# A two-layer streaming encoder: the attention accumulator of layer 1 emptied in mid-step, two cache copies and a table of biases moved to other stages

## The chip, the cores and the metric

The kernel runs on 1 core of one Trainium2 chip, as one launch. The metric is the device time of that launch in microseconds (us). The engines are called PE (TensorE), DVE (VectorE), ACT (ScalarE), POOL (GpSimd) and SP (SyncE, which only issues DMAs here); PEld is PE's loading of weights. [...]

## The reference

One inference step of a two-layer encoder over a prompt of 2048 positions and a sample of 64 positions with caches; model width 1024. Each layer is `h + rms(W_out(gated mixer(rms(h))))`.

- Layer 0 has two head groups. A is latent attention over all earlier chunks. B is attention in a band of 9 chunks of 64 positions, with a bias by clipped relative distance (a table of 8 heads x 257). Each output is multiplied by the SiLU of its gate columns, and both go into one output projection.
- Layer 1 (C) is attention in a window of 128 positions, rounded to chunks, with 16 query heads on 2 key heads, a sink per head, partial rotation and a SiLU gate.

```
o_b = _band_prompt(q_b, k_b, v_b, B_PAST_CHUNKS, B_SCALE, rel_table=rel_table)
state = (c_new, kr_new, bk, bv)      # the sample's: bk, bv = the last 512 rows of [cache, new]
o = _band_prompt(q, k, v, C_PAST_CHUNKS, C_SCALE, sinks=sinks)
return h + _rms((o * jax.nn.silu(g)) @ w_out, post_g), state
```

Of the sample's new B caches (512 rows of keys, 512 of values), 448 rows are the old caches' rows 64 to 511, unchanged. Inputs and outputs are in float32.

## The kernel before

Products are made as three matmuls of split values: a value is a high part (rounded by ACT as it empties a PSUM bank: `copy`, L211) and a low part (what is left, made by DVE: `lo_of`, L214, the "low pass"). So almost each PSUM bank is read first by ACT, then by DVE.

The program has five phases, one after another: the projections of layer 0 (phase 1, in two halves of the positions), group A's attention (2), group B's (3), the projections of layer 1 (4) and its attention (5). Output projections of a layer run beside the attention, as jobs `J` that a step pumps: `J.proj` makes the products (L964), `tail` (L985) scales by the norm (the "z pair", two DVE operations at L995) and adds the residual on POOL (L1003). The order of the work is the Tile scheduler's in phase 1 and in the first 8 steps of phase 5 (`NAUTO5`). From step 8 on PE, DVE, ACT and SP follow the order in which the code is written (`manual`, L168).

**Phase 1.** Chunks of 384 positions are loaded as x tiles of 128 rows (L253), squared on ACT (L255), scaled on DVE (L264), transposed on PE (L268) and emptied into X (L211, L214). Weights come in pieces (L226), split by ACT (L227) and DVE (L228). In the first half, after the load of W_ukv, `biases_by_distance` (L293) loads the table `rel`, stretches it on DVE (L297), stores it to DRAM (sE1, L298) and has a DMA repeat it for 128 partitions from DRAM to DRAM (sE, L299, 3072 KB). Phase 3 reads sE. At the end of phase 1 (L597) two DMAs copy the 448 unchanged rows of each B cache from DRAM to DRAM, 896 KB each. The Tile scheduler had put all of these into the first 25 us. SP issues all these DMAs; it goes round 8 semaphores, so each DMA waits until the one 8 before it has landed.

**Phase 5.** A unit is a block of 128 queries with one key group g and one parity e of heads (4 query heads); a block has four units, (0,0), (0,1), (1,0), (1,1), so 64 units in all. The blocks go in the order 8 to 15, 0 to 7. Block 0 has one key tile, the others two. `step(n)` (L1897) runs three units at different stages: scores and masks of unit n+2 (`start`: PE L1705, DVE L1708), exponentials of unit n+1 (ACT L1717), transpositions of unit n's probabilities (`turn`, PE L1726, one for each key tile b, with `copy` and `low` into PT), and the product with the values of unit n-1 (`av`, PE L1733) into the accumulator `acc`, one PSUM bank. `out` (L1813) empties it: ACT copies the lower half (tbm, L211), DVE adds the upper half (OT, L1823). For a unit (0,0), `out` first pumps jobs until at most one block is open, and takes one of the two OT buffers. After unit (1,1) `gate` (L1735) transposes the reciprocal sums (PE L1755, into the same two PSUM banks `t` as the turns), multiplies (DVE L1757, POOL L1763), and makes the operand MM of the output projection (ACT L211, then POOL's subtraction L1770).

Of the kernel before, what the change touches and what calls it, by code (L numbers as in the profile page):

```python
# [110 lines left out]
def kernel(ctx, tc, a, o, upto=5):  # L111
# [3 lines left out]
    dma = nc.sync.dma_start  # L115
# [115 lines left out]
    def mm3(ps, lhs, rhs, kt):  # L231

        n = 3 * kt
        j = 0
        for k in range(kt):
            for x, y in TERMS:
                nc.tensor.matmul(ps, lhs(x, k), rhs(y, k), start=(j == 0), stop=(j == n - 1))  # L237
                j += 1
# [38 lines left out]
    def phase1():  # L277
        with ExitStack() as st:
# [14 lines left out]
            def biases_by_distance():  # L293

                e8 = tb.tile([128, 768], F32, name="qcs")
                dma(e8[:8, 511:768], a["rel"])
                nc.vector.tensor_copy(e8[:8, 0:511], e8[:8, 511:512].to_broadcast([8, 511]))  # L297
                dma(sE1, e8[:8])  # L298
                dma(sE.rearrange("h q e -> q h e"),  # L299
                    bass.AP(tensor=sE1.tensor, offset=sE1.offset, ap=[[0, 128], [768, 8], [1, 768]]))  # L300
# [126 lines left out]
            def split_store(p, w, dst, j, c0, scale=1.0):  # L427
                hi = ev.tile([128, 512], F32R, name="ev")
                lo = ev.tile([128, 512], F32R, name="ev")
                nc.scalar.activation(hi[:, :w], p[:, :w], AF.Copy, scale=scale)  # L430
                lo_of(lo[:, :w], p[:, :w], hi[:, :w], scale)
                for x, t in ((0, hi), (1, lo)):
                    dma(head_pair(dst, x, j, c0, w), f(t[:, :w]))

            def uq(W, qT, hb, chunks):
                for c0, n in chunks:
                    def proj(j):
                        p = pm.tile([128, 512], F32, name="pm")
                        mm3(p[:, :n], lambda x, k: W[:, x, k, j * 128:(j + 1) * 128],
                            lambda y, k: qT[:, y, k, c0 - hb:c0 - hb + n], 3)  # L440
                        return p
                    for j in range(4):
                        split_store(proj(j), n, sQA, j, c0, A_SCALE)
                        yield
                    cs = tb.tile([128, 2, 384], F32, name="qcs")
                    dma(cs[:, :, :n], a["qrope"][:, :, c0:c0 + n])
                    x1, x2 = proj(4), proj(5)
                    rot_store(x1, x2, cs, n, c0, sQR, 0, 16)
                    yield

            def rot_store(x1, x2, cs, n, c0, dst, d0, hd):
                t = [ev.tile([128, 512], F32, name="ev") for _ in range(4)]
                nc.vector.tensor_mul(t[0][:, :n], x1[:, :n], cs[:, 0, :n])
                nc.vector.tensor_mul(t[1][:, :n], x2[:, :n], cs[:, 1, :n])
                nc.vector.tensor_mul(t[2][:, :n], x2[:, :n], cs[:, 0, :n])
                nc.vector.tensor_mul(t[3][:, :n], x1[:, :n], cs[:, 1, :n])
                for i, op in ((0, ALU.subtract), (1, ALU.add)):
                    u, v = t[2 * i], t[2 * i + 1]
                    nc.gpsimd.tensor_tensor(u[:, :n], u[:, :n], v[:, :n], op=op)
                    hi = ev.tile([128, 512], F32R, name="ev")  # L460
                    lo = ev.tile([128, 512], F32R, name="ev")
                    copy(hi[:, :n], u[:, :n])
                    nc.gpsimd.tensor_tensor(lo[:, :n], u[:, :n], hi[:, :n], op=ALU.subtract)
                    for x, q in ((0, hi), (1, lo)):
                        dma(dst[:, x, d0 + i * hd:d0 + (i + 1) * hd, c0:c0 + n].rearrange("h d t -> d h t"), f(q[:, :n]))
# [50 lines left out]
            def build_x(c):  # L516
                Xs[c] = x_chunk(*c)

            def fs_piece(chunks, col, specs, after=None):
                for _ in fs_steps(chunks, col, specs, after):  # L520
                    pass

            def weave(main, other, lead, rate):

                acc = 0.0
                for i, _ in enumerate(main):
                    if i >= lead - 1:
                        acc += rate
                    while acc >= 1:
                        next(other, None)  # L530
                        acc -= 1
                for _ in other:
                    pass
# [22 lines left out]
            for hf in range(2):  # L556
                chunks, hb = HALVES[hf], HBASE[hf]
                main = fs_steps(chunks, 672, kinds[0:3])
                cT = lat.tile([128, 2, 2, 1088], F32R, name="lat")
                for i, c in enumerate(chunks):  # L560
                    for _ in range(3):
                        next(main)
                    if i == 0:
                        if hf == 0:
                            later_loads()
                        W = load_w(pw, raw, w_in[:, 384:672], KT, 288, SLOT)
                    if i + 1 < len(chunks) and chunks[i + 1] not in Xs:
                        build_x(chunks[i + 1])
                    ckv(W, Xs[c], c[0], c[1], cT, hb)
                main = fs_steps(chunks, 1056, kinds[3:6])  # L570
                next(main)
                W = load_w(pw, raw, a["w_ukv"], 2, 1024, SLOT)
                if hf == 0:
                    biases_by_distance()
                weave(main, latents(W, cT, hf), LD1[hf], RT1[hf])
                W = load_w(pw, raw, w_in[:, 0:384], KT, 384, SLOT)
                qT = lat.tile([128, 2, 3, 1088], F32R, name="lat")
                for c in chunks:
                    qlat(W, Xs[c], c[0], c[1], qT, hb)
                main = fs_steps(chunks, 1440, kinds[6:9])  # L580
                next(main)
                W = load_w(pw, raw, a["w_uq"], 3, 768, SLOT)
                weave(main, uq(W, qT, hb, chunks), LD2, RT2)
                fs_piece(chunks, 1824, kinds[9:12])
                for h0 in (0, 4):
                    W = load_w(pw, raw, w_in[:, 2208 + h0 * 64:2208 + h0 * 64 + 256], KT, 256, SLOT)
                    for c in chunks:
                        vb(W, Xs[c], c[0], c[1], h0)
                Ws = [load_w(pw, raw, w_in[:, col:col + 256], KT, 256, SLOT) for col in (2720, 2976)]
                for i, c in enumerate(chunks):  # L590
                    for j in range(4, 8):
                        fs(Ws[(j - 4) // 2], Xs[c], j % 2, c[0], c[1], "g", j)
                    if hf == 0:
                        build_x(HALVES[1][i])
            dma(o[11][448:512], vbs)
            for src, dst in ((a["cache_b_k"], o[10]), (a["cache_b_v"], o[11])):
                dma(dst[0:448], src[64:512])  # L597

    def cut_keys(w):
        parts = even_split(w)  # L600
        k = len(parts)
# [1065 lines left out]
    def phase5():  # L1667

        with ExitStack() as st:
# [227 lines left out]
            def step(n):  # L1897
                cur, prv, nxt = us.get(n), us.get(n - 1), us.get(n + 1)
                if nxt:
                    nxt.exp([0, 1, 2, 3])  # L1900
                if n + 2 < len(units):
                    us[n + 2] = Unit(*units[n + 2])
                    us[n + 2].start()
                    if n % 4 == 1 and n // 4 + 2 < 16:
                        blocks[n // 4 + 2] = Block(BLOCKS5[n // 4 + 2])
                for b in range(2):
                    low = None
                    if cur and b < cur.B.nb:
                        PT, low = cur.turn(b * 128, 128)
                        cur.tasks.append(PT)  # L1910
                    pump(RATE5 / 2)
                    if low:
                        low()
                    if b == 0 and prv:
                        prv.av()
                if prv:
                    prv.out()
                    us.pop(n - 1)
                    if n % 4 == 0 and n // 4 + 1 in blocks and n > 0:
                        blocks[n // 4 + 1].load_values()  # L1920
                if not J.loaded:
                    J.load.pump(1)
                if n >= NS5:
                    J.samp.pump(1)
                if J.made < FAST5:
                    J.side.pump(SP5)
                J.rest()
# [120 lines left out]
```

## Time and profile before

| | us |
|---|---|
| median of 3 runs | 2689.81 (2688.68 to 2691.74) |
| the profiled execution's own time | 2687.59 |
| its span (first to last instruction) | 2685.8 |
| PE busy | 2562.0 (95%) |
| PEld busy | 2337.2 (87%) |
| DVE busy | 1568.8 (58%) |
| ACT busy | 1391.8 (52%) |
| POOL busy | 520.5 (19%) |

The mean granted clock is 0.988. The chain of work that ended last goes over PE for 79% of the span, DVE 9%, ACT 5%, DMA 3%. The profile is one execution; its own time is 2.2 us below the median of the runs. A row of the timeline gives the start and the length of an operation, or of several of one kind in sequence; the brackets tell how long the engine had been idle and which operation released it. Ends of matmuls are modelled.

### The profile page before, as it was taken

To read this page: it belongs to the slowest core of one execution; us is meant where nothing else is said; L and a number is where in the kernel's file an instruction comes from. 1 tells how busy PE (TensorE), PEld (TensorE's weight loads), DVE (VectorE), ACT (ScalarE), POOL (GpSimd) and SP (SyncE) were. 2 spreads that over 40 slices of the span, in tenths; PEclk is the share of its full clock that TensorE was granted. 3 is DMA by queue.
4 is the path that set the end of the run, shared out by engine and by line. 5 is a ranking of instruction groups with operands and counts; after the bars stand their busy time and mean duration, and the time that the engine had idled before them with its cause. 6 is when DMAs were issued, how large, how long until landed. Compare 5 with 4: busy or idle time off the path is not lost.

```text
span 2685.8 us, 46771 instructions
## 1 busy us (share of the span) xinstructions
PE 2562.0 (95%) x16296; PEld 2337.2 (87%) x16296; DVE 1568.8 (58%) x4299; ACT 1391.8 (52%) x3548; POOL 520.5 (19%) x1110
## 2 busy tenths in 40 slices
PE   7999999999999999999999999899999998999997
PEld 6999999899998888888778888689999998787886
DVE  6553345453227878787668776575224214787886
ACT  4332242322327777777667666553223214877773
POOL 0001000001002333221200323432001000344443
PEclk9999999999999999999999999999999999999999
DMA  7546343737537666661387776666525328555552
GB/s 243 170 152 210 124 149 113 246 111 220 173 94 201 190 180 185 175 188 49 114 243 188 201 201 177 176 233 230 152 84 176 122 72 249 118 142 135 132 133 71
DMA packets 382283, 437.94 MB, mean 163 GB/s; under 512 B 49936, under 2 KB 308888, under 8 KB 378816
## 3 DMA queue, kind: packets, MB, share of 16 engines
q1 hardware_dynamic: 382048, 434.95, 55.2%
q8 instruction: 130, 2.13, 0.3%
q14 instruction: 105, 0.86, 0.1%
HBM read 282.80 MB, written 157.09 MB: 164 GB/s over the span
## 4 chain that ended last, share of the span: by engine, by line
PE 79%; DVE 9%; ACT 5%; DMA 3%; issue 3%; POOL 1%; SPq 0%; ACTq 0%; DVEq 0%; POOLq 0%
PE pm L237 39%; PE proj L964 10%; PE s L683 6%; PE acc L754 4%; PE t L726 3%; PE acc L1228 3%; DVE PT L214 2%; PE s L1176 2%; PE t L1203 2%; PE t L1726 2%; PE acc L1733 2%; PE s L1705 1%; ACT P L702 1%; DVE m L689 1%; DVE s L1708 1%
## 5 line engine op out<-in xcount | busy, mean ns | idle before, releaser
L237 PE MATMUL pm<-X,W 128*128 128x384 f32 (+2 forms) x4536 | 754.3, 325 | 2.1 <-DVE ev L214 1.6
L237 PEld LDWEIGHTS pm<-X,W 128*128 128x128 f32 x4536 | 732.0, 189 | 5.3 <-DVE ev L214 1.9
L211 ACT ACTIVATE PT<-t 128x512 fp32r<-128x512 f32 (+3 forms) x704 | 344.1, 505 | 265.4 <-PE t L1203 76.2
L214 DVE SCALAR_TENSOR_TENSOR PT<-t,PT 128x512 fp32r<-128x512 f32 (+3 forms) x688 | 377.2, 569 | 91.6 <-ACT PT L211 89.0
L964 PE MATMUL proj<-Wo,MM 128*128 128x512 f32 (+1 forms) x1416 | 389.8, 406 | 5.0 <-ACT z L211 3.1
L214 DVE SCALAR_TENSOR_TENSOR ev<-pm,ev 128x256 fp32r<-128x256 f32 (+3 forms) x197 | 98.6, 503 | 336.0 <-ACT ev L430 101.2
L964 PEld LDWEIGHTS proj<-Wo,MM 128*128 128x128 f32 (+1 forms) x1416 | 245.2, 186 | 51.9 <-ACT z L211 6.5
L237 PE MATMUL pm<-W,X 128*128 128x256 f32 (+5 forms) x2040 | 281.2, 297 | 0.0
L237 PEld LDWEIGHTS pm<-W,X 128*128 128x128 f32 (+1 forms) x2040 | 272.0, 187 | 1.0
L702 ACT ACTIVATE P<-s,m 128x512 f32<-128x512 f32 (+9 forms) x344 | 209.5, 616 | 33.1 <-DVE m L691 30.5
L683 PE MATMUL s<-KA,Q 128*128 128x512 f32 (+7 forms) x640 | 201.4, 397 | 9.4 <-ACT P L702 8.4
L228 DVE TENSOR_TENSOR W<-R,W 128x768 fp32r<-128x768 f32 (+3 forms) x114 | 116.1, 1055 | 133.5 <-ACT W L227 133.1
L726 PE MATMUL t<-ident,P 128*128 128x128 f32 x1088 | 176.4, 276 | 3.4 <-ACT P L702 0.8
L689 DVE TENSOR_REDUCE m<-s 128x1 f32<-128x480 f32 (+7 forms) x216 | 132.4, 613 | 80.5 <-PE s L683 80.1
L726 PEld LDWEIGHTS t<-ident,P 128*128 128x128 f32 x1088 | 134.6, 141 | 41.6 <-ACT P L702 15.1
L754 PE MATMUL acc<-PT,V 128*128 128x256 f32 x1152 | 156.0, 285 | 6.5 <-DVE OT L763 6.5
L754 PEld LDWEIGHTS acc<-PT,V 128*128 128x128 f32 x1152 | 140.4, 188 | 12.0 <-PE t L726 6.0
L1717 ACT ACTIVATE P<-s,m 128x256 f32<-128x256 f32 (+2 forms) x264 | 119.6, 466 | 10.7 <-DVE m L1709 9.4
L1708 DVE CUSTOM_DVE_ANT_0 s<-s,mask 128x256 f32<-128x256 f32 (+1 forms) x256 | 107.6, 422 | 18.5 <-PE t L1726 7.7
L1228 PE MATMUL acc<-PT,V 128*128 128x256 f32 x672 | 111.5, 298 | 6.7 <-DVE OT L1238 4.5
L683 PE MATMUL s<-KR,Q 128*128 128x384 f32 (+6 forms) x320 | 116.3, 363 | 1.1 <-DMA Q<-sQR 1.1
L1180 DVE CUSTOM_DVE_ANT_0 s<-s,bias 128x640 f32<-128x640 f32 (+4 forms) x128 | 95.2, 744 | 35.1 <-PE s L1176 33.5
(251 smaller groups left out, 3941.2 us busy)
## 6 DMA issues: line engine op xcount, KB each, us to landing
Q<-sQA SPq DMA_DIRECT2D x128, 128.0 KB, 3.3
sWO<-W SPq DMA_DIRECT2D x32, 512.0 KB, 3.8
Q<-sQB SPq DMA_DIRECT2D x128, 128.0 KB, 3.3
Wo<-sWO SPq DMA_DIRECT2D x16, 1024.0 KB, 9.1
Q<-sQC SPq DMA_DIRECT2D x32, 512.0 KB, 7.2
R<-in_ab_w_in_dram SPq DMA_DIRECT2D x40, 384.0 KB, 4.0
K<-sKB SPq DMA_DIRECT2D x56, 256.0 KB, 5.4
V<-sVB SPq DMA_DIRECT2D x24, 512.0 KB, 6.3
```

The source lines that it names most:

```text
L211: nc.scalar.activation(out, in_, AF.Copy)
L214: nc.vector.scalar_tensor_tensor(out, x, scale, hi, op0=ALU.mult, op1=ALU.subtract)
L237: nc.tensor.matmul(ps, lhs(x, k), rhs(y, k), start=(j == 0), stop=(j == n - 1))
L683: nc.tensor.matmul(s[:r, :n], self.Q[:, x, self.qo:self.qo + r], rhs, start=(x == 0), stop=(x == 2))
L689: nc.vector.tensor_reduce(m[:r, j:j + 1], s[:r, :n], axis=AX.X, op=ALU.max)
L702: nc.scalar.activation(self.P[:r, o0:o0 + n], self.s.pop(j)[:r, :n], AF.Exp, bias=self.m[:r, 6:7], accum_out=acc)
L726: nc.tensor.transpose(t[:, b], self.P[:, (b0 + b) * 128:(b0 + b + 1) * 128], ident)
L754: nc.tensor.matmul(acc[:, (i // 2) % 2], H.V[:, b0 + b], PT[:, x, b], start=(b0 + b == 0 and x == 0), stop=(b0 + b == i and x == 1))
L964: nc.tensor.matmul(p, M[:, x, k, :r], W[k][:, y, cs], start=(k == k0 and t == 0), stop=(k == k1 - 1 and t == 2))
L1228: nc.tensor.matmul(acc, self.H.V[:, self.base - self.H.b0 + b], self.PT[:, x, off + b], start=(b == 0 and x == 0), stop=(b == nblk - 1 and ...
L1708: nc.vector.tensor_tensor_reduce(s[:, c, :w], s[:, c, :w], mk, 1.0, -3e38, ALU.add, ALU.max, m[:, 0, c:c + 1])
L1717: nc.scalar.activation(self.P[:, c, :w], self.s[:, c, :w], AF.Exp, bias=m[:, 1, c:c + 1], accum_out=m[:, 0, c:c + 1])
```

## The change

Three parts. First, `biases_by_distance` is called after the query up-projection of the first half (after the second `weave`), ahead of the gate pieces at column 1824. Second, the two copies of the B caches leave phase 1 and are issued in phase 5, the keys' at step 24 and the values' at step 32. Third, in `step` of phase 5, `prv.out()` stands right behind `prv.av()`, that is after the turn of key tile 0 and before that of key tile 1, instead of behind both.

```
-                if hf == 0:
-                    biases_by_distance()
                 weave(main, latents(W, cT, hf), LD1[hf], RT1[hf])
...
                 weave(main, uq(W, qT, hb, chunks), LD2, RT2)
+                if hf == 0:
+                    biases_by_distance()
                 fs_piece(chunks, 1824, kinds[9:12])
...
             dma(o[11][448:512], vbs)
-            for src, dst in ((a["cache_b_k"], o[10]), (a["cache_b_v"], o[11])):
-                dma(dst[0:448], src[64:512])
...
                     if b == 0 and prv:
                         prv.av()
+                        prv.out()
                 if prv:
-                    prv.out()
                     us.pop(n - 1)
...
+                if n in (24, 32):
+                    src, dst = (a["cache_b_k"], o[10]) if n == 24 else (a["cache_b_v"], o[11])
+                    dma(dst[0:448], src[64:512])
                 if not J.loaded:
                     J.load.pump(1)
```

In the changed kernel line numbers of phase 5 up to `step` are smaller by 3. The instructions change their places in the first part of phase 1, at the biases' new place, and in phase 5; in phases 2 to 4 they stand as before.

DVE, the end of a block in phase 5 (the step in which unit (1,1) is emptied). PT is the low pass of a turn, OT from acc the add, ri the reciprocal sums, OT from t the gate product. Before:

```order
L214 SCALAR_TENSOR_TENSOR PT_27488<-t_27483,PT_27488 128x512
L214 SCALAR_TENSOR_TENSOR PT_27507<-t_27502,PT_27507 128x512
L1823 TENSOR_TENSOR OT_27306<-acc_27497,tbm_27514 64x512
L1827 RECIPROCAL ri_27517<-rsum_26660 128x16
L1757 TENSOR_TENSOR OT_27003<-OT_27003,t_27521 128x512
```

and with the change:

```order
L214 SCALAR_TENSOR_TENSOR PT_27486<-t_27481,PT_27486 128x512
L1820 TENSOR_TENSOR OT_27290<-acc_27495,tbm_27500 64x512
L1824 RECIPROCAL ri_27503<-rsum_26658 128x16
L214 SCALAR_TENSOR_TENSOR PT_27510<-t_27505,PT_27510 128x512
L1754 TENSOR_TENSOR OT_26987<-OT_26987,t_27519 128x512
```

The add and the reciprocal stand ahead of the low pass of key tile 1 instead of behind it.

DVE, the next step, in which unit (0,0) of the following block is emptied; m is the maximum of the masked scores, z the pair of the output projection, s the masks. Before:

```order
L1709 SCALAR_TENSOR_TENSOR m_27535<-m_27535,nsink_25810 128x4
L214 SCALAR_TENSOR_TENSOR PT_27561<-t_27556,PT_27561 128x512
L214 SCALAR_TENSOR_TENSOR PT_27585<-t_27580,PT_27585 128x512
L995 SCALAR_TENSOR_TENSOR z_27117<-z_27117,rs_27370,g_post_21588 128x512 x2
L1823 TENSOR_TENSOR OT_27607<-acc_27575,tbm_27608 64x512
L1708 ISA s_27618,m_27619<-s_27618,mask_25802 128x256
```

and with the change:

```order
L1706 SCALAR_TENSOR_TENSOR m_27533<-m_27533,nsink_25808 128x4
L214 SCALAR_TENSOR_TENSOR PT_27559<-t_27554,PT_27559 128x512
L992 SCALAR_TENSOR_TENSOR z_27115<-z_27115,rs_27368,g_post_21586 128x512 x2
L1820 TENSOR_TENSOR OT_27591<-acc_27573,tbm_27592 64x512
L214 SCALAR_TENSOR_TENSOR PT_27600<-t_27595,PT_27600 128x512
L1705 ISA s_27616,m_27617<-s_27616,mask_25800 128x256
```

The z pair and the add have moved ahead of the low pass of key tile 1.

ACT, the start of phase 1: X_126 is the first chunk, emptied from the transpositions pt; W_227 and W_331 are the first two weights; sq_348 is the square of the next chunk's first x tile. Before:

```order
L211 ACTIVATE X_126<-pt_184 128x4x128
L211 ACTIVATE X_126<-pt_191 128x4x128
L227 ACTIVATE W_227<-R_236 128x768
L227 ACTIVATE W_227<-R_240 128x768
L211 ACTIVATE X_126<-pt_212 128x4x128
L211 ACTIVATE X_126<-pt_219 128x4x128
L227 ACTIVATE W_331<-R_332 128x864
L227 ACTIVATE W_331<-R_336 128x864
L227 ACTIVATE W_331<-R_340 128x576
L255 ACTIVATE sq_348,ss3_345<-R_346 128x1024
```

and with the change:

```order
L227 ACTIVATE W_227<-R_236 128x768
L227 ACTIVATE W_227<-R_240 128x768
L227 ACTIVATE W_331<-R_332 128x864
L211 ACTIVATE X_126<-pt_184 128x4x128
L211 ACTIVATE X_126<-pt_191 128x4x128
L227 ACTIVATE W_331<-R_336 128x864
L227 ACTIVATE W_331<-R_340 128x576
L255 ACTIVATE sq_348,ss3_345<-R_346 128x1024
L211 ACTIVATE X_126<-pt_212 128x4x128
L211 ACTIVATE X_126<-pt_219 128x4x128
```

The last two pieces of the first chunk (from pt_212 and pt_219) stand behind all pieces of W_331 and behind the square of the next x tile; PE's first product with the first weight waits for the piece from pt_212 in both.

## Rows read from the trace of the kernel before

**Rows 1.** The windows of the kernel before, one stretch of 40 us in phase 5: length; busy time of PE, PE's weight loads, DVE, ACT and POOL with their instructions; the granted clock of PE as a share of full speed; the DMA engines' busy share; GB/s.

```profile
2400.00:2440.00 40.00, 38.33 (x227) 32.50 (x226) 34.80 (x85) 30.97 (x90) 19.87 (x35) 1.00 0.59 143
```

**Rows 2.** The waits of PE between 2300 and 2640 us: what waited, for what, and then us in total, times, longest.

```profile
PE acc L1733 <- DVE OT L1823: 13.2, 14, 3.8
```

**Rows 3.** The timeline of PE in phase 5: start, length, line, operation, tiles, shape, count; in brackets the idle time before and what ended it. The first matmul of an accumulator.

```profile
2388.05 1.17 PE L1733 MATMUL acc<-PT,VC 128*128 128x512 f32 x4 [0.72 <-DVE OT L1823]
...
2412.39 1.17 PE L1733 MATMUL acc<-PT,VC 128*128 128x512 f32 x4 [0.74 <-DVE OT L1823]
...
2462.43 0.73 PE L1733 MATMUL acc<-PT,VC 128*128 128x512 f32 x2 [3.85 <-DVE OT L1823]
...
2631.84 1.16 PE L1733 MATMUL acc<-PT,VC 128*128 128x512 f32 x4 [1.65 <-DVE OT L1823]
...
2636.17 1.16 PE L1733 MATMUL acc<-PT,VC 128*128 128x512 f32 x4 [0.20 <-DVE OT L1823]
```

**Rows 4.** The timeline of DVE around the wait of 2412.39, columns as in rows 3.

```profile
2401.48 0.69 DVE L214 SCALAR_TENSOR_TENSOR PT<-t,PT 128x512 fp32r<-128x512 f32 x1 [0.94 <-ACT PT L211]
...
2402.79 0.68 DVE L1823 TENSOR_TENSOR OT<-acc,tbm 64x512 f32<-64x512 f32 x1 [0.62 <-ACT tbm L211]
...
2403.50 0.25 DVE L1827 RECIPROCAL ri<-rsum 128x16 f32<-128x16 f32 x1
...
2406.72 1.44 DVE L214 SCALAR_TENSOR_TENSOR PT<-t,PT 128x512 fp32r<-128x512 f32 x2
...
2408.08 3.57 DVE L995 SCALAR_TENSOR_TENSOR z<-z,rs,g_post 128x512 f32<-128x512 f32 x2
...
2411.57 0.68 DVE L1823 TENSOR_TENSOR OT<-acc,tbm 64x512 f32<-64x512 f32 x1
...
2412.17 0.41 DVE L1708 CUSTOM_DVE_ANT_0 s<-s,mask 128x256 f32<-128x256 f32 x1
...
2414.33 1.28 DVE L214 SCALAR_TENSOR_TENSOR PT<-t,PT 128x512 fp32r<-128x512 f32 x2
```

**Rows 5.** The timeline of ACT in the same stretch.

```profile
2400.84 0.60 ACT L211 ACTIVATE PT<-t 128x512 fp32r<-128x512 f32 x1 [2.11 <-PE t L1726]
...
2402.16 0.59 ACT L211 ACTIVATE tbm<-acc 64x512 f32<-64x512 f32 x1
...
2407.33 1.05 ACT L211 ACTIVATE MM<-OT 128x1024 fp32r<-128x1024 f32 x1
```

**Rows 6.** The timeline of POOL in the same stretch.

```profile
2404.38 2.40 POOL L1763 TENSOR_TENSOR OT<-OT,G 128x1024 f32<-128x1024 f32 x1 [4.17 <-DVE OT L1757]
...
2408.46 2.64 POOL L1770 TENSOR_TENSOR MM<-OT,MM 128x1024 fp32r<-128x1024 f32 x1 [1.37 <-ACT MM L211]
```

**Rows 7.** The timeline of PE in the same stretch.

```profile
2399.29 1.08 PE L1733 MATMUL acc<-PT,VC 128*128 128x512 f32 x4
...
2402.73 0.60 PE L1726 MATMUL t<-ident,P 128*128 128x128 f32 x4
...
2413.75 1.19 PE L1705 MATMUL s<-KC,Q 128*128 128x256 f32 x8
```

**Rows 8.** The timeline of DVE (its first row) and POOL before the wait of 2462.43, where the block of the first 128 positions begins.

```profile
2450.68 0.69 DVE L1823 TENSOR_TENSOR OT<-acc,tbm 64x512 f32<-64x512 f32 x1 [2.40 <-PE s L1705]
...
2456.93 2.37 POOL L1003 TENSOR_TENSOR x<-z,x 128x1024 f32<-128x1024 f32 x1 [1.72 <-DVE z L995]
...
2459.26 2.40 POOL L1770 TENSOR_TENSOR MM<-OT,MM 128x1024 fp32r<-128x1024 f32 x1
```

**Rows 9.** The timeline of PE at the last unit of phase 5.

```profile
2640.81 1.08 PE L1733 MATMUL acc<-PT,VC 128*128 128x512 f32 x4
...
2644.66 5.56 PE L964 MATMUL acc<-Wo,MM 128*128 128x512 f32 x23 [1.65 <-DVE OT L1823]
```

**Rows 10.** The DMA issues of the first 30 us: what, queue, count, KB each, median us from issue to landing.

```profile
out_dram<-in_cache_b_k_dram SPq DMA_DIRECT2D x1, 896.0 KB, 8.4
...
sE<-sE SPq DMA_DIRECT2D x1, 3072.0 KB, 14.4
...
R<-in_x_prompt_dram SPq DMA_DIRECT2D x8, 512.0 KB, 5.9
...
R<-in_ab_w_in_dram SPq DMA_DIRECT2D x1, 288.0 KB, 2.8
```

**Rows 11.** The timeline of ACT (its first two rows) and PE in the first 55 us.

```profile
21.25 1.12 ACT L211 ACTIVATE X<-pt 128x512 fp32r<-128x512 f32 x2
...
26.03 1.06 ACT L255 ACTIVATE sq<-R 128x1024 bf16<-128x1024 f32 x1 [0.89 <-DMA R<-in_x_prompt_dram]
...
21.88 14.84 PE L237 MATMUL pm<-X,W 128*128 128x384 f32 x72
...
36.56 9.75 PE L237 MATMUL pm<-W,X 128*128 128x288 f32 x72
...
47.54 1.07 PE L268 MATMUL pt<-ident,R 128*128 128x128 f32 x8 [1.23 <-DVE R L264]
...
50.34 0.47 PE L389 MATMUL po<-ident,k 128*128 128x128 f32 x1 [1.73 <-POOL k L381]
...
55.00 1.01 PE L237 MATMUL pm<-X,W 128*128 128x384 f32 x2
```

**Rows 12.** The windows again, two microseconds of the start; columns as in rows 1.

```profile
50.00:52.00 2.00, 1.67 (x7) 1.52 (x8) 1.90 (x7) 0.46 (x2) 0.26 (x1) 0.50 0.58 186
```

More of the change, by code (lines that the diff above doesn't have):

```diff
@@ L572, in phase1 @@
                 W = load_w(pw, raw, a["w_ukv"], 2, 1024, SLOT)
-                if hf == 0:
-                    biases_by_distance()
                 weave(main, latents(W, cT, hf), LD1[hf], RT1[hf])
@@ L583, in phase1 @@
                 weave(main, uq(W, qT, hb, chunks), LD2, RT2)
+                if hf == 0:
+                    biases_by_distance()
                 fs_piece(chunks, 1824, kinds[9:12])
@@ L595, in phase1 @@
             dma(o[11][448:512], vbs)
-            for src, dst in ((a["cache_b_k"], o[10]), (a["cache_b_v"], o[11])):
-                dma(dst[0:448], src[64:512])
     def cut_keys(w):
@@ L1915, in step @@
                         prv.av()
+                        prv.out()
                 if prv:
-                    prv.out()
                     us.pop(n - 1)
@@ L1920, in step @@
                         blocks[n // 4 + 1].load_values()
+                if n in (24, 32):
+                    src, dst = (a["cache_b_k"], o[10]) if n == 24 else (a["cache_b_v"], o[11])
+                    dma(dst[0:448], src[64:512])
                 if not J.loaded:
```

## The prediction

> **What bounds the kernel now.** I read the windows first: in a steady stretch of layer 1's attention PE is busy 38.33 of 40 us, DVE 34.80, ACT 30.97, and the DMA engines 0.59 of the time [rows 1]. So PE sets the pace, with DVE close behind; the reader should see that nothing can be won here but PE's 1.67 idle microseconds. Then the waits of PE: between 2300 and 2640 us it waited 14 times for the add that empties the accumulator (OT L1823), 13.2 us in all [rows 2]. The timeline places them: 0.72 at 2388.05 and 0.74 at 2412.39 are two of the regular ones, one in each block of four units; 3.85 at 2462.43, 1.65 at 2631.84 and 0.20 at 2636.17 are special [rows 3]. Without these three, 7.5 us over 11 blocks is left. Then the rows of DVE, ACT, POOL and PE around one such wait [rows 4 to 7] give the chain behind it, and last the DMA issues and the first 55 us, where the copies and the biases are.
>
> In the chain the wait is not made by the accumulator alone. When unit (0,0) is due, DVE is busy without a gap from the low pass at 2406.72 to the low pass at 2414.33, with the z pair of the output projection (3.57 us) ahead of the add [rows 4]. So a mid-step add helps only if DVE's whole chain starts earlier. That has to be worked out.
>
> **The mid-step add, an ordinary end of block.** Before, DVE stood idle 0.94 us before low pass 1 (2401.48) and 0.62 before the add (2402.79) [rows 4], since ACT makes the second PT (2400.84) and then z before tbm (2402.16) [rows 5], though the accumulator was complete at 2399.29 + 1.08 = 2400.37 [rows 7]. With the new order tbm (0.60) runs 2400.40 to 2401.00, the add starts at 2401.04, the reciprocal 0.71 later, low pass 1 another 0.17 later, at 2401.92, and ends 0.69 later, at 2402.61. PE's next transposition, at 2402.73 [rows 7], needs it: 0.12 us to spare. Before, the three were through at 2403.50 + 0.17 = 2403.67: 1.06 later. I count 0.9 of it, since the masks behind also need PE's scores. So DVE's chain runs 0.9 us earlier, because idle time in front of the add is now used.
>
> [...] The reciprocal began 0.71 after an add of 0.68, where the mask behind the add of 2411.57 began 0.60 after one of 0.68 [rows 4]: the add of odd e, which writes partitions 64 to 127, lets nothing overlap behind it. [...]
>
> **The next unit, (0,0).** POOL's gate product (2.40) begins at 2403.4 instead of 2404.38 [rows 6], ending 2405.8; low pass 0 then begins about 2405.85 instead of 2406.72, the z pair about 2406.5 instead of 2408.08 since low pass 1 now stands behind it. ACT's MM copy (1.05, before at 2407.33 [rows 5]) goes 2405.85 to 2406.9, and POOL's subtraction (2.64) 2406.9 to 2409.5. Beside it the z pair takes its 3.57 as before, to 2410.1; the add ends at 2410.75. PE comes to the accumulator at 2412.39 - 0.74 = 2411.65: no wait. Low pass 1 (2411.4), four masks and the small op (2411.57 + 0.60 to 2414.33 is 2.16 [rows 4]) bring low pass 0 to 2413.6, done 2414.25. PE's transposition, which needs it, would be due at 2413.75 + 1.19 - 0.74 = 2414.20 [rows 7]. So the wait goes nearly whole, and DVE is level with PE after it. Bounds of one block: 0 and 0.74. I take 0.64, the working with 0.05 to 0.1 lost: **11 blocks, -7.0** (0 to -7.5).
>
> **The block with one key tile.** At 2462.43 the add waited for POOL's subtraction, which stands behind POOL's residual add of 2456.93 and began only at 2459.26 [rows 8]. The order on POOL stays so. But the add of 2450.68 had been held 2.40 us (ACT made z before tbm), and all that follows (gate product, MM, masks, low pass, z pair, residual add) hangs on it. With tbm first it comes about 1.5 earlier. **-1.5** (0 to -3.85, if the whole wait went).
>
> **The end.** The waits at 2631.84 and 2636.17 hang on the same chain and lose the 0.9 by which it leads and the 0.20. The last accumulator is complete at 2640.81 + 1.08 = 2641.89, yet PE waited 1.65 for its add, until 2644.66 [rows 9]: tbm stood behind z, which stood behind PE's last products. New: tbm (0.60) and the add (0.68) end at 2643.2; PE starts 1.4 earlier. **-2.5** (-1 to -3.5).
>
> **Steps 0 to 7** are ordered by the scheduler, and PE waits there for several things in turn; I take 0 and put 3 us both ways into the range.
>
> **The copies.** They take SP issue and DMA time out of the first 20 us and put it where the DMA engines are busy 0.59 of the time [rows 1]. At the start one landed 8.4 us after issue [rows 10]. In the new place the loads behind them are for a block that starts about 24 us later (2388.05 to 2412.39 [rows 3] is 24.34). Cover: one block; cost 0, up to +2 if a gate or value load came late.
>
> **The biases.** At their new place the broadcast of 3072 KB (14.4 us [rows 10]) has three gate pieces beside it: 72 matmuls of 14.84 us [rows 11]. The store that waits for the eighth DMA back meets a broadcast nearly landed. Cost 0 (to +1). The 3 MB and the copies no longer compete with the first x tiles.
>
> **The first 55 us.** Before, first matmuls at 21.88, then 14.84 and 9.75 us of them, then PE idle 1.23 and 1.73 because the tiles of the next chunk came late [rows 11], and the clock fell to half (0.50 in 50 to 52 [rows 12]). Now the tiles come early, and all three go. But ACT's order is worse: the last two evacuations of the first chunk stood at 21.25, ahead of three pieces of weights and the square of the next x (26.03 [rows 11]); now they stand behind them. That x is issued when DVE has taken the fourth piece of weights, by the lengths of the pieces at about 20, and lands in 2.8 us (the 288 KB piece) to 5.9 (the median of x [rows 10]); with the square (1.06, and its sum) and one copy (0.56) the first matmul comes at 24.6 to 27.7, about 26, instead of 21.88. PE then has 14.84 + 9.75 + 24 transpositions (3.2, at 1.07 for 8 [rows 11]) = 27.8 us without a gap: 53.8, against 55.0 before [rows 11]. **-1** (-4 to +3).
>
> **Sum.** -7.0 - 1.5 - 2.5 - 1 = -12.0 on the profiled 2687.59 us: 2675.6. The median of the runs shown is 2.2 above that execution, so I forecast **2678**.
>
> **Rivals.**
> - DVE takes over (0.24). Low pass 1 behind the add makes DVE late for the transposition bank, and the 0.74 comes back as a wait on PT L214 in each block. For it: my working leaves DVE level with PE. Against: 0.94 + 0.62 us of idle DVE ahead of each chain. Then only -1.5 - 2.5 - 1 is left: 2685, no measurable change (0.2%, 5.4 us, is about what a measurement of this kernel can tell).
> - All of it (0.12): also the block with one key tile and the start in full (-3.85 and -4): 2689.8 - 7 - 3.85 - 2.5 - 4 = 2672.
> - Slower (0.11): in the two steps of a block with a gate transposition, PE needs low pass 1 in the same step, and I left 0.12 us. It decides from there: if the add starts later than 2401.16 (tbm taken only after the second PT, or after z, as ACT did before), low pass 1 ends up to 1.3 later, PE waits up to 1.2. At 0.6 each, 24 steps give +14, and with -5 of the other terms: about 2699.
> - The change may not do what it says for the start: the earlier x tile gains nothing if ACT's new order holds PE as long as the stall did. That is inside the -4 to +3.
>
> **Numbers.** Forecast 0.53, and 0.12 for all of it: faster 0.65. DVE takes over: same 0.24. Slower 0.11. The range from 2670 to 2692 holds the first three with the bounds of start and steps 0 to 7; the forecast's own is 2672 to 2684.
>
> **What would show it.** The rows PE acc <- DVE OT should fall from 13.2 to about 3 us between 2300 and 2640, with no row PE t <- DVE PT of more than 2 us in their place; blocks 23.6 us long instead of 24.4; the z pair still near 3.57. PE idle at 46 to 51 gone, first L237 row near 26, no half clock there. Wrong if low pass 1 shows as PE's releaser once or twice a block, or if the first chunk ends after 57.

## The result and the profile after

The changed kernel takes **2671.97 us** (median of 4 runs, 2671.28 to 2678.40) against 2690.09 of the kernel before in the same set of runs (4 runs, 2688.68 to 2691.74): ratio 0.9937, 95% interval [0.9922, 0.9953]. Its profiled execution took 2672.01 us, 15.6 less than the 2687.59 of before; the span is 2670.2 and the mean granted clock 0.992 (before 0.988).

First the page: the busy times in all.

```profile
PE 2551.1 (96%) x16296; PEld 2333.8 (87%) x16296; DVE 1569.1 (59%) x4299; ACT 1387.7 (52%) x3548; POOL 518.9 (19%) x1110
```

DVE, ACT and POOL do what they did. The time came out of PE's waits. The windows of the stretch of [rows 1], and the two microseconds of [rows 12]:

```profile
2400.00:2440.00 40.00, 40.00 (x239) 34.57 (x238) 36.63 (x97) 33.89 (x103) 21.14 (x44) 1.00 0.71 174
50.00:52.00 2.00, 2.00 (x18) 2.00 (x16) 1.94 (x9) 0.90 (x3) 0.26 (x1) 1.00 0.41 52
```

PE is busy for all of the 40 us (before 38.33), and full speed is granted at 50 to 52 us. The waits of PE between 2300 and 2640 us, as in [rows 2]: one single wait of `av`'s product for the accumulator is left, and the transposition bank has not taken its place.

```profile
PE acc L1730 <- DVE OT L1820: 2.4, 1, 2.4
...
PE t L1723 <- DVE PT L214: 0.7, 2, 0.4
PE t L1752 <- DVE PT L214: 0.6, 1, 0.6
```

Now PE's timeline round a regular block [rows 3, 7], then the product after the block with one key tile, and the first product of the output projection after the last unit [rows 9].

```profile
2387.72 1.08 PE L1730 MATMUL acc<-PT,VC 128*128 128x512 f32 x4
...
2398.63 1.08 PE L1730 MATMUL acc<-PT,VC 128*128 128x512 f32 x4
...
2402.07 0.60 PE L1723 MATMUL t<-ident,P 128*128 128x128 f32 x4
...
2410.03 0.93 PE L961 MATMUL proj<-Wo,MM 128*128 128x512 f32 x3
2410.80 1.08 PE L1730 MATMUL acc<-PT,VC 128*128 128x512 f32 x4
2411.73 0.60 PE L1723 MATMUL t<-ident,P 128*128 128x128 f32 x4
2412.08 1.20 PE L1702 MATMUL s<-KC,Q 128*128 128x256 f32 x8
2413.17 0.66 PE L1723 MATMUL t<-ident,P 128*128 128x128 f32 x4
...
2457.81 0.73 PE L1730 MATMUL acc<-PT,VC 128*128 128x512 f32 x2 [2.37 <-DVE OT L1820]
...
2629.06 1.21 PE L961 MATMUL acc<-Wo,MM 128*128 128x512 f32 x4 [0.27 <-DVE OT L1820]
```

A block lasts 2410.80 - 2387.72 = 23.08 us instead of 24.34, and no bracket stands in it. DVE's timeline of the same place, answering [rows 4]:

```profile
2400.44 0.68 DVE L1820 TENSOR_TENSOR OT<-acc,tbm 64x512 f32<-64x512 f32 x1 [0.56 <-ACT tbm L211]
2401.14 0.25 DVE L1824 RECIPROCAL ri<-rsum 128x16 f32<-128x16 f32 x1
2401.31 0.63 DVE L214 SCALAR_TENSOR_TENSOR PT<-t,PT 128x512 fp32r<-128x512 f32 x1
...
2404.95 0.68 DVE L214 SCALAR_TENSOR_TENSOR PT<-t,PT 128x512 fp32r<-128x512 f32 x1
2405.55 3.60 DVE L992 SCALAR_TENSOR_TENSOR z<-z,rs,g_post 128x512 f32<-128x512 f32 x2
2409.07 0.67 DVE L1820 TENSOR_TENSOR OT<-acc,tbm 64x512 f32<-64x512 f32 x1
2409.67 0.67 DVE L214 SCALAR_TENSOR_TENSOR PT<-t,PT 128x512 fp32r<-128x512 f32 x1
...
2412.43 0.68 DVE L214 SCALAR_TENSOR_TENSOR PT<-t,PT 128x512 fp32r<-128x512 f32 x1
```

ACT's and POOL's, answering [rows 5] and [rows 6]:

```profile
2399.81 0.59 ACT L211 ACTIVATE tbm<-acc 64x512 f32<-64x512 f32 x1 [1.76 <-PE acc L1730]
2400.43 0.60 ACT L211 ACTIVATE PT<-t 128x512 fp32r<-128x512 f32 x1
...
2405.04 1.06 ACT L211 ACTIVATE MM<-OT 128x1024 fp32r<-128x1024 f32 x1 [0.51 <-POOL OT L1760]
```

```profile
2402.60 2.40 POOL L1760 TENSOR_TENSOR OT<-OT,G 128x1024 f32<-128x1024 f32 x1 [3.05 <-DVE OT L1754]
...
2406.18 2.42 POOL L1767 TENSOR_TENSOR MM<-OT,MM 128x1024 fp32r<-128x1024 f32 x1 [0.87 <-ACT MM L211]
```

ACT takes tbm at once when the accumulator is complete, ahead of the second PT. The one idle time left ahead of DVE's add (0.56) is the copy of tbm itself. PE in the first 55 us, answering [rows 11], and then ACT:

```profile
26.71 1.33 PE L237 MATMUL pm<-X,W 128*128 128x384 f32 x3 [3.21 <-ACT X L211]
...
54.48 0.61 PE L237 MATMUL pm<-X,W 128*128 128x384 f32 x2
```

```profile
25.03 1.06 ACT L255 ACTIVATE sq<-R 128x1024 bf16<-128x1024 f32 x1 [0.67 <-DMA R<-in_x_prompt_dram]
...
26.08 1.06 ACT L211 ACTIVATE X<-pt 128x512 fp32r<-128x512 f32 x2
```

The first product starts at 26.71 instead of 21.88, since the last two evacuations of the first chunk stand behind the square of the next x. From there PE has no gap, and the chunk's end comes at 54.48 instead of 55.00.

**Where the time is.** I set each PE instruction of the changed trace against the same one of before and read how its start moved. "To 137 us" ends at the 700th instruction. "137 to 2240 us" is the rest of phase 1, with the biases' new place, and phases 2 to 4. "Steps 0 to 7" goes from there to the product of unit 12, counted from 1 (2325.86 before).

| stage | forecast | changed kernel |
|---|---|---|
| to 137 us | -1 | -1.2 |
| 137 to 2240 us | 0 | +3.9 |
| steps 0 to 7 | 0 (±3) | +0.2 |
| 11 regular blocks | -7.0 | -13.5 |
| block with one key tile | -1.5 | -1.5 |
| the end, with the tail | -2.5 | -3.5 |
| sum | -12.0 | -15.6 |

From 137 to 2240 us PE and ACT have the same instructions in the same order in both kernels. DVE's order differs at the biases' new place, from 151 to 256 us, and there PE's shift stays at -1.2. Stretches at a lower granted clock fall at other places in the two executions. One window (columns as in [rows 1]) shows it, first before, then the changed kernel:

```profile
1360.00:1380.00 20.00, 19.87 (x131) 15.76 (x130) 13.26 (x38) 13.12 (x35) 2.05 (x5) 1.00 0.76 227
```

```profile
1360.00:1380.00 20.00, 19.87 (x122) 15.79 (x121) 12.40 (x36) 11.34 (x29) 0.81 (x4) 0.91 0.59 186
```

Here the changed kernel has the lower granted clock (0.91 to 1.00); from 1320 to 1340 us it is the kernel before (0.84 to 1.00). Over the whole 137 to 2240 us the mean granted clock is 0.990 before and 0.994 in the changed kernel, so the clock doesn't account for the +3.9, and its cause stays open. It is no larger than what executions differ by without a change: e6 below, in which PE, DVE and ACT keep the order of the kernel before up to 2240 us, gains 4.0 us in the same stretch. So the share of phase 5 (-18.3) is read from its own stage.

### The profile page after: what moved, and what is told of

It reads as the page before. It is cut to its first block, busy times and chain, and to the rows that moved or that the text cites. A ratio compares the mean times of both kernels' runs of the same rounds, so it can differ in the third digit from the quotient of the medians.

```text
span 2670.2 us, 46749 instructions
## 1 busy us (share of the span) xinstructions
PE 2551.1 (96%) x16296; PEld 2333.8 (87%) x16296; DVE 1569.1 (59%) x4299; ACT 1387.7 (52%) x3548; POOL 518.9 (19%) x1110
## 4 chain that ended last, share of the span: by engine, by line
PE 81%; DVE 7%; ACT 5%; DMA 3%; issue 2%; POOL 1%; SPq 0%; ACTq 0%; DVEq 0%; POOLq 0%
PE pm L237 39%; PE proj L961 11%; PE s L680 6%; PE acc L751 4%; PE t L723 3%; PE acc L1225 3%; PE s L1702 2%; PE t L1200 2%; PE acc L1730 2%; PE s L1173 2%; PE t L1723 2%; DVE PT L214 2%; ACT P L699 1%; DVE m L686 1%; ACT PT L211 1%
## 5 line engine op out<-in xcount | busy, mean ns | idle before, releaser
L227 ACT ACTIVATE W<-R 128x768 fp32r<-128x768 f32 (+3 forms) x114 | 98.3, 909 | 33.8 <-DMA R<-in_ab_w_in_dram 19.3
```

## The experiments

All ratios are against the kernel before, run on the same chip in the same set of runs. "Block" is the mean change of a block's length over units 42 to 58, "12 to 64" the change of the stretch from unit 12's product to unit 64's (314.95 us before), both from one trace of each run, with units counted from 1. The changed kernel has -1.24 and -17.1.

| run | us | ratio, 95% interval | block | 12 to 64 |
|---|---|---|---|---|
| e1 mid-step alone | 2670.23 | 0.9919 [0.9897, 0.9941] | -1.25 | -18.6 |
| e2 copies and biases alone | 2692.00 | 1.0005 [0.9995, 1.0014] | +0.01 | +0.2 |
| e3 only tbm in mid-step | 2688.93 | 0.9990 [0.9980, 1.0000] | +0.18 | +0.1 |
| e4 z pair behind the add | 2683.97 | 0.9973 [0.9958, 0.9989] | +0.02 | -4.2 |
| e5 mid-step for (0,0) | 2689.68 | 0.9994 [0.9984, 1.0004] | -0.12 | -2.1 |
| e6 mid-step for (1,1) | 2688.14 | 0.9982 [0.9972, 0.9993] | -0.01 | -1.8 |
| e9 both, (0,0) and (1,1) | 2674.90 | 0.9944 [0.9930, 0.9957] | -1.15 | -17.5 |
| e7 mid-step, biases | 2664.98 | 0.9902 [0.9883, 0.9922] | -1.25 | -18.7 |
| e8 mid-step, copies | 2670.91 | 0.9921 [0.9904, 0.9938] | -1.25 | -18.6 |
| e10 as e7, tail 2 calls later | 2664.41 | 0.9907 [0.9892, 0.9923] | -0.69 | -15.4 |
| e11 as e7, tail 3 calls later | 2663.41 | 0.9898 [0.9879, 0.9916] | -1.01 | -18.3 |

**Which part of the change.** e1 has the third part of the diff alone, e2 the first two.

e1: 

> The kernel before with the mid-step emptying alone; biases and copies stay at the start. Theory A (DVE's chain at each block's end starts earlier, and both stalls of PE behind it go): each of the 11 regular blocks of phase 5 shorter by about 1.2 us (0.9 at the accumulator, 0.3 at the following transposition), the block with one key tile by 1.5, the end by 3.5, so 16 to 18 us less than before, about 2672 to 2674. Theory B (part of the gain of the whole change comes from the copies and the biases leaving the start): 11 to 13 us less, about 2678.

e2: 

> The kernel before with the biases and the two copies moved and the emptying left at the end of the step. Theory A: only the first 55 us change, by about -1.2 us, so the ratio is not distinguishable from 1 (2688 to 2690). Theory B: 4 to 6 us less. In both, the first product of PE comes near 26.7 instead of 21.9, and the stall at 46 to 51 us is gone.

The emptying in mid-step carries the whole gain: e1 is as fast as the change, and in e2 the blocks stay as they were. The trace of e2 wins 1.8 us at the start but loses 5.7 in steps 0 to 7. The scheduler's order is not the reason: it differs from that of the kernel before only from 2280 us on, and e2 has lost 5.3 by 2260. The granted clock differs there. The windows show it, first before, then e2:

```profile
2246.00:2256.00 10.00, 8.09 (x55) 7.25 (x54) 7.38 (x24) 5.11 (x16) 0.60 (x3) 1.00 0.86 196
...
2246.00:2256.00 10.00, 7.63 (x34) 6.55 (x33) 6.47 (x19) 3.79 (x10) 0.40 (x2) 0.69 0.70 172
```

PE gets through 34 matmuls instead of 55. e5 loses 6.4 us in the same steps, with the order of the kernel before until 2310 us; e3, which leaves the copies and the biases where they were, is granted 0.83 in this window and gets through 37 matmuls; the changed kernel, which moves the same copies and biases as e2, is granted 1.00 there and loses 0.2. So this loss belongs to the execution and not to the moved copies and biases; what lowers the clock in some executions is not shown.

**Is it the copy of tbm, the z pair, or the order?** e3 takes only ACT's copy forward and leaves DVE's add at the step's end. e4 leaves the emptying as before and makes the output projection's tail wait three calls more, so that the z pair stands behind the add.

```
# e3: in Unit
+ def tb(self):
+     self.tbm = sc.tile([64, 512], F32, name="tbm", bufs=2)
+     copy(self.tbm, self.acc[64:128])
...
# out() adds self.tbm; in step:
                     if b == 0 and prv:
                         prv.av()
+                        prv.tb()
...
# e4: in tail, J.lag = 3 in phase 5 (0 elsewhere)
                 yield
+                for _ in range(J.lag):
+                    yield
             for c in range(2):
```

e3: 

> The kernel before with only ACT's copy of the lower half (tbm) moved to mid-step; DVE's add stays behind both low passes. If the add was late because ACT made z and the second PT before tbm (theory A1), DVE's add at a block's end comes about 0.7 us earlier, which removes most of the 0.9 and the 0.3 of a block: 8 to 12 us less, 2678 to 2682. If the order on DVE is what counts, the add ahead of the second low pass (theory A2), nearly nothing changes in the regular blocks and only the end gains about 1.5: 2687 to 2689.

e4: 

> The kernel before with the tail of the output projection three calls later in phase 5, so that in the step of unit (0,0) both operations of the z pair stand behind the add instead of ahead of it. If the z pair on DVE is what holds the add (theory Z), the add follows the second low pass at once, and 0.7 or more of each block's 1.2 goes: 8 us or more less, 2682 or lower. If POOL's subtraction, which frees the second OT buffer, ends the add's wait anyway (theory P), the add comes only about 0.4 earlier (POOL ended at 2411.10, the add began at 2411.57) and the DVE work behind it is as long: 0 to 4 us less, 2686 to 2690.

e3 gains nothing in the blocks, as its second theory (A2) has it. Waits of PE from 2300 to 2640, and DVE's rows of step (0,0):

```profile
PE acc L1733 <- DVE OT L1826: 12.3, 13, 2.4
PE t L1726 <- DVE PT L214: 2.9, 10, 1.2
```

```profile
2410.34 0.69 DVE L214 SCALAR_TENSOR_TENSOR PT<-t,PT 128x512 fp32r<-128x512 f32 x1 [0.59 <-ACT PT L211]
2410.95 3.57 DVE L995 SCALAR_TENSOR_TENSOR z<-z,rs,g_post 128x512 f32<-128x512 f32 x2
2414.45 0.67 DVE L1826 TENSOR_TENSOR OT<-acc,tbm 64x512 f32<-64x512 f32 x1
```

Low pass 1 stands ahead of the z pair and waits for ACT's second PT, and so for PE's second turn of that very step: DVE stands idle 0.59 there, and gets no further ahead of PE in this step than this row lets it.

e4 has the z pair out of the way, yet its waits only change their name:

```profile
PE t L1730 <- DVE PT L214: 8.0, 11, 0.8
PE acc L1737 <- DVE OT L1827: 2.1, 4, 1.0
```

```profile
2406.05 1.42 DVE L214 SCALAR_TENSOR_TENSOR PT<-t,PT 128x512 fp32r<-128x512 f32 x2
2410.22 0.68 DVE L1827 TENSOR_TENSOR OT<-acc,tbm 64x512 f32<-64x512 f32 x1 [2.76 <-POOL MM L1774]
```

The add now waits 2.76 us for POOL's subtraction, which frees the OT buffer that unit (0,0) takes, and what DVE does behind the add is as late for the transposition bank as it was for the accumulator. Of e4's -4.2, 3.1 come from the block with one key tile. With 2.2 more behind unit 64 its 2683.97 lies below what theory P gave, though the steady blocks (+0.02) are as that theory has them.

**Which of the four units of a block.** The edit is a condition on the unit: `prv.out()` in mid-step where it holds, else after both turns.

```
                     if b == 0 and prv:
                         prv.av()
+                        if COND:        # e5: prv.g + prv.e == 0
+                            prv.out()   # e6: prv.g + prv.e == 2; e9: prv.g == prv.e
                 if prv:
-                    prv.out()
+                    if not COND:
+                        prv.out()
```

e5: 

> Only the units (0,0) are emptied in mid-step, the other three of a block after both turns; copies and biases as before. Theory L (the prediction's chain: DVE's row of work has to start earlier at a block's end, in the step that empties unit (1,1)): the z pair and the add go ahead of low pass 1 in step (0,0), so PE's wait for the accumulator goes, but DVE's row is no shorter, low pass 0 of the next turn still ends near 0.9 us before where it did, and the stall comes back at the transposition bank as in the run with the z pair behind the add: at most -0.3 us a block, 2685 to 2692 in all. Rival F (it is the order in that one step that counts, since two low-pass positions behind the z pair held the add): -0.9 us or more a block, 2674 to 2679.

e6: 

> Only the units (1,1), the last of each block, are emptied in mid-step; (0,0), (0,1) and (1,0) after both turns as before. Theory L: the add and the reciprocal go ahead of low pass 1, the gate product and all behind it come 0.9 us earlier, and the wait of 0.74 in step (0,0) goes with it: -0.7 to -1.2 us a block, also -1.5 at the block with one key tile and -2 to -3.5 at the end: 2672 to 2679. Rival F: -0.3 us or less a block, only the block with one key tile and the end gain: 2684 to 2688.

e9: 

> The units (0,0) and (1,1) are emptied in mid-step, (0,1) and (1,0) after both turns; copies and biases as before. Theory L and F together (in step (1,1) DVE's row comes 0.9 us forward; in step (0,0) the z pair and the add must stand ahead of low pass 1, which waits for PE's own second turn, or the row stops there; either alone gave 0.0 and -0.1 us a block): both at once give -0.9 to -1.25 us a block, 2670 to 2675 in all. Rival M (all four units of a block have to be emptied in mid-step, because the lead of DVE has to be carried through (0,1) and (1,0)): -0.5 us or less a block, 2679 to 2688.

e5 came as theory L has it (-0.12 a block). e6 did not (-0.01 a block for -0.7 to -1.2), and tells most. DVE's and PE's rows of e6:

```profile
2401.81 0.69 DVE L1823 TENSOR_TENSOR OT<-acc,tbm 64x512 f32<-64x512 f32 x1 [0.56 <-ACT tbm L211]
...
2406.34 0.68 DVE L214 SCALAR_TENSOR_TENSOR PT<-t,PT 128x512 fp32r<-128x512 f32 x1
2408.18 0.69 DVE L214 SCALAR_TENSOR_TENSOR PT<-t,PT 128x512 fp32r<-128x512 f32 x1 [1.17 <-ACT PT L211]
2408.79 3.56 DVE L995 SCALAR_TENSOR_TENSOR z<-z,rs,g_post 128x512 f32<-128x512 f32 x2
2412.28 0.67 DVE L1823 TENSOR_TENSOR OT<-acc,tbm 64x512 f32<-64x512 f32 x1
```

```profile
2413.09 1.17 PE L1733 MATMUL acc<-PT,VC 128*128 128x512 f32 x4 [0.71 <-DVE OT L1823]
```

The rows of e6 are 0.70 us later than those of before here. The add of unit (1,1) comes 2402.79 + 0.70 - 2401.81 = 1.68 earlier and low pass 0 of the next step 1.08 earlier: DVE has the lead that the prediction counted on. Then low pass 1 stands idle 1.17 for ACT's second PT, the lead is gone, and PE waits 0.71 where it waited 0.74. In e5 it is the other way: the accumulator's wait of the block is gone (-0.8), but DVE's row starts no earlier, and the next step's transposition waits for the low pass:

```profile
PE t L1726 <- DVE PT L214: 9.0, 11, 1.5
```

-0.8 and +0.7: -0.12 a block. With both, e9 gives -1.15. The parts gain 0.0 and 0.1 alone and 1.15 together; (0,1) and (1,0) add the last 0.1. e9 also keeps the gain at the end (its last accumulator waits 0.3 instead of 1.65).

**Copies and biases apart**, each with the emptying in mid-step.

e7: 

> Mid-step emptying and the biases moved, the copies left at the end of phase 1 as before. ACT's order of the first 25 us has all evacuations of the first chunk ahead of the third and fourth pieces of weights. Theory B (the 3 MB repeat of the biases made the second chunk's tiles late and ACT's order, not the transfers, made the first matmul late in the changed kernel): first matmul near 22 us, no idle at 46 to 51 us, the end of the first chunk at 50 to 52 us, so 2 to 4 us less than the mid-step change alone (2670.2): 2666 to 2669. Rival C (the two copies were what made the tiles late): the idle at 46 to 51 stays, first chunk's end at 55, 2669 to 2672.

e8: 

> Mid-step emptying and the copies moved into phase 5, the biases left where they were. Theory B: the second chunk's tiles are late as before, first chunk's end at 54 to 56 us; the copies in phase 5 cost nothing: 2669 to 2672. Rival C: idle at 46 to 51 gone, first chunk's end at 51 to 54 us, 2667 to 2669. If the copies cost something in phase 5, the blocks of steps 24 to 40 are longer by 0.5 to 2 us in all than with the mid-step change alone.

The biases moved alone win 6.8 us to 137 us, the copies alone 1.8, both together (the change) 1.2. Each is one trace: e10 and e11, which start as e7 does, win 5.5 and 8.0, and the runs that start as the kernel before does lie between -0.6 and +0.7. PE's first product in e7, with ACT ahead of it:

```profile
22.16 14.51 PE L237 MATMUL pm<-X,W 128*128 128x384 f32 x72 [0.72 <-ACT X L211]
```

```profile
21.53 1.07 ACT L211 ACTIVATE X<-pt 128x512 fp32r<-128x512 f32 x2
```

There ACT keeps the evacuations ahead of the weights and the square, PE starts at 22.16, and the later idle times of [rows 11] are gone as well. My expectation had the mechanism and too small a size (2 to 4 us): the first product comes 26.71 - 22.16 = 4.55 us earlier than in the changed kernel, and nothing later gives that back. For e8 I had expected the tiles of the second chunk late as before, with the chunk's end at 54 to 56 us. Its median (2670.91) is in the range given with that, but the trace shows what the rival said:

```profile
53.48 1.12 PE L237 MATMUL pm<-X,W 128*128 128x384 f32 x3
```

PE has no wait of more than 0.2 us between 46 and 52 us there. Either move alone takes away the idle times of 1.23 and 1.73. In phase 5 the copies cost nothing that the trace shows: e8's stretch from unit 12 to 64 is as short as e1's, to 0.1 us.

**Can the rest go too?** e10 and e11 are e7 with J.lag = 2 and 3.

e10: 

> Mid-step emptying and biases moved, and in phase 5 the output projection's tail two calls later: one z operation before the add and one behind low pass 1, POOL's residual add behind its MM subtraction in the block with one key tile. If the 2.4 us wait left there is made by that residual add alone, it goes, and the steady blocks stay as they are: 2660 to 2664. Rival: the z operation that now stands ahead of the masks delays the scores' masks and the next low pass, PE waits for the transposition bank in each block: 2665 to 2672.

e11: 

> As the run before, with the tail three calls later: the add stands directly behind low pass 0 and both z operations behind low pass 1. By the chain of the steady block (low pass 0, add, low pass 1, a z operation, masks) the add could come 3.6 us earlier, which nobody waits for any more; the next low pass 0 comes no later than now: same as the run before within 2 us, 2660 to 2666. Rival: POOL's subtraction (2.4 us, begun at the MM copy) holds the add through the second OT buffer as in the run with the z pair behind, and low pass 1 queued behind it is late by 1 to 2 us: PE waits for the transposition bank, 2668 to 2685.

The wait at the block with one key tile goes in both (-4.0 there, -1.5 in the change), but the steady blocks give it back: they gain 0.69 and 1.01 instead of 1.25, over 11 blocks about 6 and 3 us less. In e10, with one z operation between low pass 1 and the masks, PE waits 12 times for a low pass between 2290 and 2630 us, 5.4 us in all. In both runs the add waits for POOL's subtraction (2.35 us in e10, 3.00 in e11); why e11 loses less is not taken apart here. In their ratios both are even with e7. e7 is the version to keep: its interval ends at 0.9922, where the change's begins. From e1 (0.9919) the runs don't part it.

## Why the prediction was right, and which size was wrong

The forecast was 2678 with 2672 to 2684 as its own range; the median of 2671.97 lies at the lower end of that range, inside 2670 to 2692. In the profiled execution that is partly luck: the blocks and the end gave 7.5 us more than forecast, and the +3.9 from 137 to 2240 us, which no term of the sum had, hid half of it.

**The mechanism held, row by row.** The changed trace at this place is 0.66 us ahead (2399.29 in [rows 7] is 2398.63). With 0.66 added, the working and the trace:

| | worked out | measured |
|---|---|---|
| tbm begins | 2400.40 | 2400.47 |
| add of (1,1) begins | 2401.04 | 2401.10 |
| low pass 1 ends | 2402.61 | 2402.60 |
| PE's transposition that needs it | 2402.73 | 2402.73 |
| gate product on POOL begins | 2403.4 | 2403.26 |
| MM copy begins | 2405.85 | 2405.70 |
| z pair begins | 2406.5 | 2406.21 |
| add of (0,0) ends | 2410.75 | 2410.40 |
| PE comes to the accumulator | 2411.65 | 2411.46 |
| low pass 0 ends | 2414.25 | 2413.77 |
| PE's transposition that needs it | 2414.20 | 2413.83 |

The spare of 0.12 ahead of low pass 1, on which the slower rival hung, was 0.13. DVE is level with PE at the block's end, as forecast: low pass 0 ends 0.06 before PE's transposition. The working had both things in it that e5 and e6 take apart, the earlier row and the order in step (0,0), though it named only the first as the cause ("only if DVE's whole chain starts earlier"). e6 shows that the first alone is worth nothing in a regular block.

**The term that was mis-sized: the regular blocks**, 0.64 worked out, 13.5 / 11 = 1.23 measured. The step that failed is that PE's transposition "would be due at 2413.75 + 1.19 - 0.74 = 2414.20", with 0.74 as the block's upper bound. Two things were missed.

- An idle time of 0.74 costs more than 0.74. In the changed trace PE doesn't wait here, and the product starts before the modelled end of the group ahead: that end is 2410.03 + 0.93 = 2410.96, the start 2410.80, 0.16 earlier. The row with the bracket has lost that overlap too, and 0.74 + 0.16 = 0.90 is what the starts show (-0.9 at each such product).
- There was a second stall without a bracket. Before, the transpositions ahead of the scores of 2413.75 and behind them were:

```profile
2413.40 0.60 PE L1726 MATMUL t<-ident,P 128*128 128x128 f32 x4
...
2415.07 0.66 PE L1726 MATMUL t<-ident,P 128*128 128x128 f32 x4
```

The second is 1.32 after the scores' start, where the changed trace has 2413.17 - 2412.08 = 1.09. PE waited there for the low pass that [rows 4] has at 2414.33; with 0.08 between the product and the next transposition (2413.40 - 2412.39 = 1.01, now 2411.73 - 2410.80 = 0.93) this is the other 0.3 of a block. In the other three steps of a regular block the transposition follows the scores' start by 0.96 to 1.04, in both kernels.

**The other steps.** The block with one key tile: -1.5 forecast and measured; POOL's residual add still stands ahead of its subtraction, and 2.37 us of wait are left. The end: -3.5 instead of -2.5, at the edge given; the wait of 1.65 is 0.27 now, that of 1.65 at 2631.84 is gone. The start: -1.2 for -1, with the first product at 26.71 for "about 26" and the chunk's end at 54.48 for 53.8. It came out as two opposite effects, which e7 and e8 now separate. The copies: 0 and 0. The biases at their new place: 0 and 0, PE's shift is -1.2 at 137 us and at 260. SP's waits in the trace of before show the distance of eight that this term goes by: the 10th issue waits 1.0 us for the 2nd, the 16th 0.6 for the 8th, the 17th 0.2 for the 9th. Steps 0 to 7: +0.2 here, but from -0.4 (e1) to +6.4 (e5) over the runs; ±3 was too narrow for that stage.

**The start behind the add on DVE.** The operation behind the add of odd e starts 2401.14 - 2400.44 = 0.70 after it, the one behind the add of even e 2409.67 - 2409.07 = 0.60: the difference of the kernel before stands. No wait of PE came of it, since low pass 1 still ended 0.13 before PE needed it. What makes the difference, no run here shows.

**The rivals.** DVE takes over: no, PE waits 1.3 us in all for low passes in those 340 us. It is what e5 and e4 look like. Slower by low pass 1: not seen. All of it: the time is that rival's (2672), but not by its way; the wait of the block with one key tile stayed, and the start gave 1.2.

## What to carry to other kernels

Read a stall's price from the starts of the same instructions with and without it (0.90 here), not from the idle time in its row (0.74), and look at the spacing of the unbracketed rows behind it for a second one. In e6 DVE, in the written order, got ahead only as far as its first instruction that waited for PE by way of ACT: its low pass 0 came 1.08 us earlier, then low pass 1 stood idle 1.17. Bring such a row forward and also put that instruction behind the work that must be early, since here the two alone were worth 0.0 and 0.1 us a block and both 1.15. Two moves that each free the start of a program can undo each other through the scheduler's order (6.8 and 1.8 us alone, 1.2 together); time them apart. Before giving a difference of one stage to the change, look at what that stage does in runs that left it alone: here, from 137 to 2240 us, that was up to 4 us.

## What the runs showed that I had not expected

The wait of 2.4 us behind the block with one key tile was followed by different clocks in different executions. The changed kernel (wait 2.37) and e1 (wait 2.38), 5 us that begin about 3 us after it:

```profile
2461.00:2466.00 5.00, 5.00 (x23) 4.07 (x22) 3.96 (x15) 4.23 (x17) 2.52 (x14) 0.83 0.29 107
```

```profile
2458.00:2463.00 5.00, 5.00 (x32) 4.34 (x31) 4.80 (x16) 4.94 (x21) 2.52 (x14) 1.00 0.28 98
```

23 matmuls against 32 in 5 us at the same place. This is why e1 has -18.6 from unit 12 to 64 and the change -17.1, with equal blocks. What decides it, no run here tells.
